# A state space stage reordered: ticks of small products and half a dense tile, with TensorE's order given by the source

## The chip, the cores and the metric

The kernel runs on one core of one Trainium2 chip. The metric is the device time of one execution in microseconds (us), as a median of several. Engines are named as the profile names them: PE (TensorE, the matrix unit), PEld (its weight loads), DVE (VectorE), ACT (ScalarE), POOL (GpSimd) and SP (the queue that issues nearly all DMA transfers). Differences under 0.2% can't be told from no change here.

## The reference

One layer of a decoder: a Mamba-2 state space branch and a sparse attention branch, joined by gates, then a squared-ReLU MLP, for a prompt of 16 + 512 tokens and for 8 decode sequences of 8 tokens each. The change concerns the state space branch and the projections that stand beside it:

```python
u = rmsnorm(h, norm1_w)
z, xbc, dt_raw, q, k, v, qi, ki, wi, g_ssm, g_attn = split_in(u @ w_in)
xbc, conv_state = causal_conv(xbc_raw, conv_prefix, conv_w, conv_b)   # width 4, then silu
...
def step(h, inp):                       # one chunk of 128 tokens, 4 groups of 8 heads
    xc, dc, bc, cc = inp
    acum = jnp.cumsum(dc * a_h, axis=1)
    decay = jnp.exp(jnp.where(causal, seg, -jnp.inf))
    cb = jnp.einsum('bign,bjgn->bijg', cc, bc)
    y = jnp.einsum('bijg,bijge,bjgep->bigep', cb, decay, xdt)
    y = y + jnp.einsum('bign,bgepn->bigep', cc, h) * jnp.exp(acum)[..., None]
    h = h * jnp.exp(last)[..., None, None] + jnp.einsum('bjge,bjgep,bjgn->bgepn', wj, xdt, bc)
...
y = (y + xs * d_skip) * jax.nn.silu(z)  # then a norm per group, times ssm_norm_w
merged = jax.nn.sigmoid(g_ssm) * (y_ssm @ w_ssm_proj) + jax.nn.sigmoid(g_attn) * (y_att @ w_attn_proj)
```

The decode sequences run the same recurrence from a given state (8 sequences, 32 heads, 64 x 128 each), which is read, used and written back updated.

## The kernel before

The 576 tokens and the 16 meta tokens lie in SBUF as normed activations split into a high and a low part (`uh`, `ul`, 8 x 128 rows of 592 columns). A dense tile is one block of 128 output columns of `w_in`: its weights come by DMA into `wr` (two buffers), ACT makes the high part `wh` (L128), POOL the low part `wl` by a subtraction (L129), and PE makes 2 halves of 24 products each (`mm3`, L151: 8 blocks of the contraction, three products high x high, low x high, high x low), one bank of PSUM (tag `w`, two banks) for each half of the columns.

Order: the order in which the source writes instructions gives priorities, and a scheduler of the framework then sets the order of every engine's instructions, and of SP's transfers, when the kernel is built. Each engine then runs its own list in order.

The stage in question makes, for each of four groups g of heads:

- six convolution tiles (`conv_tile`: B, C and four x tiles): the dense tile, copies by ACT into `rb` (L572 to L575), three multiply-adds by DVE (L588), tanh by ACT, two products by DVE (L593, L596), a scaled copy by ACT, transposes by PE (L608, L611), and stores to DRAM scratch (`d_bc`, `d_xd`, `d_x`, `d_b`);
- four `z` tiles (`z_tile`, silu by ACT and DVE L562, stored to `d_z`);
- `start(g)`: loads of that group's B, C and decode rows;
- four `states(g, i)`: a block `st` of decode states of 512 KB is loaded, transposed by PE (L682), multiplied by C (L690) and updated by POOL (L684), PE (L698) and DVE (L700);
- five `chunk(g, c)`, four of the prompt and one (c = 4) for decode and meta tokens: `bc` is loaded from `d_ac` by a broadcasting DMA and turned into the decay by ACT (L729, L731), PE makes the mask product (L734), DVE `cb` (L736) and eight products `bc` = decay x dt x cb (L741); PE makes the eight L743, the four L757 and the state update L768; then comes a chain DVE (L762, L763), POOL (L773), DVE (L774), ACT (L776), POOL (L777, L778), PE (L782), DVE and POOL (L160, L161, the root), DVE (L786), PE (L789), DVE (L791) and a store to `d_y`.

`Pipe` runs the units as generators: units of the next group's tiles are pushed beside the states and chunks of this group, first four states, then five chunks. `top_s()` (32 rounds of MAX8 and MATCH_REPLACE, L535 and L536, of a top-256) advances by two rounds beside each of these. `together` makes the first of a set of products wait for the operands of all of them. After the loop over groups, 16 gate tiles (`gate`, dense tiles with a tanh) follow, and then the next stage, attention on the decode sequences, with gathers of cached keys (`Kg`, L859) and the projection of `d_y` (`yw`, L1040).

## Time and profile before

| | us |
|---|---|
| median of 3 runs | 1550.33 |
| their range | 1547.67 to 1550.42 |
| the profiled execution | 1541.95 |
| its span, first to last instruction | 1540.2 |

| stage by its work | from to (us) | PE busy | DVE busy | POOL busy |
|---|---|---|---|---|
| up to the first convolution tiles | 0 to 165 | 143.6 | 135.9 | 54.4 |
| state space stage and gates | 165 to 745 | 522.5 | 405.8 | 329.0 |
| attention and merge | 745 to 1000 | 245.3 | 177.6 | 137.0 |
| output projection and MLP | 1000 to 1540 | 517.2 | 285.5 | 195.1 |

Busy time is the time in which the engine had an instruction in work. Matmuls overlap in the pipeline, so PE's busy time does not tell how far it is from its pace. A line such as `L151 PE MATMUL ... x915 | 282.1, 308 | 15.9 <-ACT rb L572` names line, engine, operation, count, busy time in us, mean ns of one, and the idle time ahead with what ended it. In the chain of waits each row has a start, a length and what took it.

### The profile page before, as it was taken

The numbers are of one execution on the slowest core, as the hardware profiler recorded it, in microseconds if no ns is written. First come the engines' busy times: TensorE is split into PE (matmuls) and PEld (weight loads), VectorE is DVE, ScalarE is ACT, GpSimd is POOL, SyncE is SP. The second block draws the span as 40 slices with busy tenths as digits, with TensorE's granted clock in tenths as the row PEclk, the third lists the DMA queues.
The fourth block names the chain that finished last, engine by engine and source line by source line (L and its number), as shares of the span: only waits on it lengthen the run. The fifth ranks groups of instructions, "written<-read, shape, count | busy, mean of one in ns | idle before, by whom it ended". The sixth has DMA issues, their size and how long they took to land.

```text
span 1540.2 us, 26573 instructions
## 1 busy us (share of the span) xinstructions
PE 1428.6 (93%) x9960; PEld 1290.4 (84%) x9960; DVE 1004.8 (65%) x1905; ACT 664.1 (43%) x1484; POOL 715.4 (46%) x644
## 2 busy tenths in 40 slices
PE   6899999888888898889899999989998999999998
PEld 6888989878878888779788887887897998899886
DVE  5799999878768676461444788864565644564444
ACT  4463445455555465443565565522342321232211
POOL 3422343647656566555445765244254533352322
PEclk9999999999999999999999999999999999999999
DMA  6424555786876877867984432035233312332212
GB/s 184 105 56 112 165 150 149 222 228 168 239 212 186 240 210 182 246 174 213 314 264 156 142 100 79 17 121 178 62 96 110 110 56 69 96 96 67 71 41 69
DMA packets 297609, 221.55 MB, mean 144 GB/s; under 512 B 43820, under 2 KB 267360, under 8 KB 297456
## 3 DMA queue, kind: packets, MB, share of 16 engines
q1 hardware_dynamic: 292232, 200.98, 46.1%
q0 software_dynamic: 5248, 18.88, 3.5%
q8 instruction: 78, 1.28, 0.3%
q14 instruction: 51, 0.42, 0.1%
HBM read 174.97 MB, written 44.07 MB: 142 GB/s over the span
## 4 chain that ended last, share of the span: by engine, by line
PE 51%; DVE 19%; DMA 13%; issue 6%; ACT 6%; POOL 4%; SPq 2%; POOLq 0%; DVEq 0%; ACTq 0%
PE s L1194 13%; PE w L151 12%; PE a L151 10%; PE w L1057 5%; DMA bc<-d_ac 3%; DVE ca L588 2%; DMA wr<-in_w_up_dram 2%; POOL wl L129 2%; DVE scs L536 2%; DVE m8s L535 2%; DVE bc L741 1%; DVE r L1218 1%; ACT wh L128 1%; DVE am L365 1%; DMA d_x<-tk 1%
## 5 line engine op out<-in xcount | busy, mean ns | idle before, releaser
L129 POOL TENSOR_TENSOR wl<-wr,wh 128x1024 fp32r<-128x1024 f32 x128 | 312.1, 2438 | 335.1 <-ACT wh L128 311.5
L151 PE MATMUL w<-uh,wh 128*128 128x288 f32 (+1 forms) x1168 | 360.6, 309 | 21.6 <-ACT rb L572 7.4
L151 PE MATMUL w<-ul,wh 128*128 128x288 f32 (+1 forms) x1168 | 355.7, 305 | 0.6 <-DVE ul L220 0.6
L151 PE MATMUL w<-uh,wl 128*128 128x288 f32 (+1 forms) x1168 | 355.0, 304 | 0.0
L151 PEld LDWEIGHTS w<-uh,wh 128*128 128x128 f32 x1168 | 224.8, 192 | 30.0 <-ACT rb L572 8.6
L151 PEld LDWEIGHTS w<-ul,wh 128*128 128x128 f32 x1168 | 224.9, 193 | 4.5 <-issue 2.9
L151 PEld LDWEIGHTS w<-uh,wl 128*128 128x128 f32 x1168 | 223.6, 191 | 2.1 <-issue 1.4
L128 ACT ACTIVATE wh<-wr 128x1024 fp32r<-128x1024 f32 x129 | 136.2, 1056 | 115.3 <-PE w L151 55.5
L129 POOL TENSOR_TENSOR dl<-wr,dh 128x1024 fp32r<-128x1024 f32 x40 | 99.0, 2477 | 158.1 <-ACT dh L128 157.9
L151 PE MATMUL a<-u2h,wh 128*128 128x288 f32 (+2 forms) x512 | 151.5, 296 | 1.0 <-ACT r L1217 1.0
L151 PE MATMUL a<-u2l,wh 128*128 128x288 f32 (+2 forms) x512 | 151.2, 296 | 0.0
L151 PE MATMUL a<-u2h,wl 128*128 128x288 f32 (+2 forms) x512 | 151.1, 295 | 0.0
L1196 DVE TENSOR_TENSOR h<-h,s 128x512 f32<-128x512 f32 (+1 forms) x101 | 67.3, 679 | 124.6 <-PE s L1194 124.2
L1194 PE MATMUL s<-dh,hh 128*128 128x512 f32 (+1 forms) x324 | 127.6, 395 | 6.3 <-DVE h L1196 6.3
L1194 PE MATMUL s<-dl,hh 128*128 128x512 f32 (+1 forms) x324 | 127.3, 394 | 0.0
L588 DVE SCALAR_TENSOR_TENSOR ca<-rb,cwT,ca 128x616 f32<-128x616 f32 x72 | 96.0, 1334 | 22.9 <-ACT ca L586 22.4
L1218 DVE TENSOR_TENSOR r<-r 128x288 f32<-128x288 f32 (+2 forms) x64 | 74.4, 1163 | 52.9 <-ACT r L1217 52.9
L128 ACT ACTIVATE dh<-wr 128x1024 fp32r<-128x1024 f32 x40 | 42.3, 1058 | 152.3 <-PE s L1194 131.3
L1194 PE MATMUL s<-dh,hl 128*128 128x512 f32 (+1 forms) x260 | 102.5, 394 | 0.0
L151 PEld LDWEIGHTS a<-u2h,wh 128*128 128x128 f32 x512 | 96.1, 188 | 2.1 <-ACT r L1217 1.5
L151 PEld LDWEIGHTS a<-u2l,wh 128*128 128x128 f32 x512 | 96.1, 188 | 0.7
L151 PEld LDWEIGHTS a<-u2h,wl 128*128 128x128 f32 x512 | 96.1, 188 | 0.0
(378 smaller groups left out, 3263.5 us busy)
## 6 DMA issues: line engine op xcount, KB each, us to landing
wr<-in_w_in_dram SPq DMA_DIRECT2D x64, 512.0 KB
wr<-in_w_up_dram SPq DMA_DIRECT2D x32, 512.0 KB
wr<-in_w_down_dram SPq DMA_DIRECT2D x32, 512.0 KB
st<-in_state_ssm_dram SPq DMA_DIRECT2D x16, 512.0 KB
bc<-d_ac SPq DMA_DIRECT2D x32, 256.0 KB
out_dram<-st SPq DMA_DIRECT2D x16, 512.0 KB
wr<-in_w_ssm_proj_dram SPq DMA_DIRECT2D x16, 512.0 KB
d_xd<-th SPq DMA_DIRECT2D x16, 296.0 KB
```

The costliest lines, as they stand in the source:

```text
L128: act.activation(hi, raw, AF.Copy)
L129: (lo_eng or pool).tensor_tensor(lo, raw, hi.bitcast(FT), op=OP.subtract)
L151: pe.matmul(ps[:, :c1 - c0], p[:, k, :], x[:, c0:c1], start=(k == 0 and i == 0), stop=(k == 7 and i == 2))
L365: dve.scalar_tensor_tensor(sc, r[:, :L], wis[:, t, h:h + 1], sc, op0=OP.mult, op1=OP.add)
L535: dve.max(m8, scs)
L536: dve.match_replace(scs, m8, scs, MARK)
L588: dve.scalar_tensor_tensor(ca[:, 0:616], rb[:, k:k + 616], cwT[:, 24 * k + ct:24 * k + ct + 1], ca[:, 0:616], op0=OP.mult, op1=OP.add)
L741: end = dve.scalar_tensor_tensor(mt, mt, dts[:n, c, 8 * g + hh:8 * g + hh + 1], cb[:n, :n], op0=OP.mult, op1=OP.mult)
L1057: pe.matmul(ps[:, :HQ], p[:, k, mc], x[k][:, c0:c1], start=(k == 0 and i == 0), stop=(k == 3 and i == 2))
L1194: pe.matmul(ps, x, w[:, cc], start=(k == 0 and i == 0), stop=(k == len(ws) - 1 and i == len(terms) - 1))
L1196: dve.tensor_tensor(h2[:, t, cc], h2[:, t, cc], ps, op=OP.add)
L1218: dve.tensor_tensor(r, r, r, op=OP.mult)
```

## The change

`inproj` of the tiles of this stage is cut in two by a new generator `dense`: weights are asked for (`w_load`), split two ticks later (`w_split`), and two ticks after that come the two halves, one in each tick, each evacuated by ACT right behind its 24 products. The loop counts ticks. In each tick first all running `states`, `chunk` and `start` units advance by a step, then the tiles whose step is not a half tile, then the one that has a half tile. A new tile starts every second tick, in the order conv and z of the four groups, then the 16 gates. The scan of group g begins at tick 33 + 20 g, with a new unit each second tick, in the order state, chunk, state, chunk, and so on, and `chunk(g, 3)` last. Inside the stage PE's instructions keep the order of the source (`manual_schedule` for PE alone); the other engines and SP's queue are still ordered by the scheduler. `together` is gone here. Loads are issued one to three ticks before their use, stores one or two ticks after their data. `top_s` yields after every round, two ticks in three up to tick 30 and one in four after. The meta tokens' state moves from `chunk(g, 4)` to `start(g)`, `cb` and `rd` share three buffers.

```diff
+    def dense(cols, n, evac):
+        raw = w_load(in_cols(cols))
+        yield from wait(2)
+        w = w_split(raw)
+        yield from wait(2)
+        for h in range(2):
+            ps = pst("w")
+            mm3(ps, w, uh, ul, h * n, h * n + n)
+            evac(h, ps)
+            yield
...
     with tc.tile_pool(name="p3", bufs=1, reuse_waits="tile") as p3, \
-            tc.tile_pool(name="p3s", bufs=1, reuse_waits="tile") as p3s:
+            tc.tile_pool(name="p3s", bufs=1, reuse_waits="tile") as p3s, \
+            tc.manual_schedule(engines={mybir.EngineType.PE}):
...
         def chunk(g, c):
...
-                sy.dma_start(bc[:n, :, :n], d_ac[None, h0:h0 + 4, 128 * c:128 * c + n].to_broadcast([n, 4, n]))
+                sy.dma_start(bc[:n, :, :n], d_ac[None, h0:h0 + 4, tok].to_broadcast([n, 4, n]))
+            yield from wait(2)
+            xd, EB = [p3.tile([128, 4, 128], FT, tag=x, name=x, bufs=2) for x in ("xd", "EB")]
...
+            for q, bc in enumerate(bcs):
                 for i in range(4):
                     act.activation(bc[:n, i, :n], bc[:n, i, :n], AF.Relu, scale=-1.0,
...
-            yield
-            py = pst("s")
             mts = [bcs[hh // 4][:n, hh % 4, :n] for hh in range(8)]
             for hh, mt in enumerate(mts):
-                end = dve.scalar_tensor_tensor(mt, mt, dts[:n, c, 8 * g + hh:8 * g + hh + 1], cb[:n, :n], op0=OP.mult, op1=OP.mult)
-            for hh, mt in enumerate(mts):
-                mm = pe.matmul(py[64 * (hh % 2):64 * (hh % 2) + 64, 128 * (hh // 2):128 * (hh // 2) + n],
-                               xt[:n, 64 * hh:64 * hh + 64], mt, start=True, stop=True)
-                if hh == 0:
-                    together(mm, [end])
+                dve.scalar_tensor_tensor(mt, mt, dts[:n, c, 8 * g + hh:8 * g + hh + 1], cb[:n, :n], op0=OP.mult, op1=OP.mult)
...
+            yield
...
+            py = pst("s")
+            for hh, mt in enumerate(mts):
+                pe.matmul(py[64 * (hh % 2):64 * (hh % 2) + 64, 128 * (hh // 2):128 * (hh // 2) + n],
+                          xt[:n, 64 * hh:64 * hh + 64], mt, start=True, stop=True)
...
+        line = []
+        for g in range(4):
             c = [conv_tile(ct) for ct in (16 + g, 20 + g, 4 * g, 4 * g + 1, 4 * g + 2, 4 * g + 3)]
             z = [z_tile(4 * g + j) for j in range(4)]
-            return [c[0], c[1], z[0], c[2], z[1], c[3], z[2], c[4], z[3], c[5]]
+            line += [c[0], c[1], c[2], z[0], c[3], z[1], c[4], z[2], c[5], z[3]]
+        line += [gate(gt, m) for gt in (0, 1) for m in range(8)]
+        scans = {}
+        for g in range(4):
+            base = 33 + 20 * g
+            scans.setdefault(base - 3, []).append(start(g))
+            for j, u in enumerate((states(g, 0), chunk(g, 0), states(g, 1), chunk(g, 1), states(g, 2), chunk(g, 2),
+                                   states(g, 3), chunk(g, 4), chunk(g, 3))):
+                scans.setdefault(base + 2 * j, []).append(u)
...
+        while line or scan or run or scans:
+            scan += scans.pop(tick, [])
+            scan = [u for u in scan if next(u, u) is not u]
+            if line and tick % 2 == 0:
+                run.append([-1, line.pop(0)])
+            for late in (False, True):
+                for x in run:
+                    if (x[0] + 1 in DENSE) == late and x[1] is not None:
+                        if next(x[1], x) is x:
+                            x[1] = None
+            run = [[x[0] + 1, x[1]] for x in run if x[1] is not None]
+            if tick % 3 < 2 if tick < 30 else tick % 4 == 0:
                 next(tops, None)
+            tick += 1
```

The count of matmuls on PE is the same in both programs. Line numbers after the change are larger: L626 stands for L588, L639 for L593, L811 and L814 for L736 and L741, L830 for L743, L851 for L782, L858 for L789, L865 for L798, L935 for L859, L1133 for L1057, L157 and L134 for L151 and L136.

What DVE has in its list around the end of the top-k, before (L535 and L536 are its rounds, L541 and L545 what follows the last one, L700 the update of a state, L736 the first chunk):

```order
L535 MAX m8s<-scs 128x8
L593 SCALAR_TENSOR_TENSOR rb<-th,ca 128x528
L596 SCALAR_TENSOR_TENSOR rb<-th,ca 128x64
L588 SCALAR_TENSOR_TENSOR ca<-rb,cwT,ca 128x616
L536 MATCH_REPLACE scs<-m8s,scs 128x1032
L588 SCALAR_TENSOR_TENSOR ca<-rb,cwT,ca 128x616
L541 TENSOR_SCALAR nm<-scs 128x8
L545 TENSOR_SCALAR scs<-scs 128x1024
L562 SCALAR_TENSOR_TENSOR zt<-zt,zl 128x576
```

And after, at the same place (L541 and L542 are the rounds now, L546 and L550 what follows them):

```order
L639 SCALAR_TENSOR_TENSOR rb<-th,ca 128x528
L642 SCALAR_TENSOR_TENSOR rb<-th,ca 128x64
L542 MATCH_REPLACE scs<-m8s,scs 128x1032
L541 MAX m8s<-scs 128x8
L542 MATCH_REPLACE scs<-m8s,scs 128x1032
L546 TENSOR_SCALAR nm<-scs 128x8
L550 TENSOR_SCALAR scs<-scs 128x1024
L547 TENSOR_TENSOR nm_6543<-nm,cst 128x64
```

All 32 rounds stand ahead of the first chunk in both lists, with 6 tiles through L593 (L639) by the last round in both; between there and the first `cb` stand 3 more before and 4 more after.

DVE at a chunk in the middle of the stage, before: after the eight products (L741) come convolution steps of the next group, one after the other, with the chain of two chunks between them.

```order
L736 TENSOR_TENSOR cb<-a,cst 128x128
L741 SCALAR_TENSOR_TENSOR bc<-bc,dts,cb 128x128 x8
L786 TENSOR_SCALAR rd<-cst,ss 128x128
L791 SCALAR_TENSOR_TENSOR y_3741<-y_3741,nwT,a 128x128 x4
L160 TENSOR_SCALAR ss<-a 128x1
L588 SCALAR_TENSOR_TENSOR ca<-rb,cwT,ca 128x616
L762 TENSOR_TENSOR y_4068<-s,EB 128x512
L588 SCALAR_TENSOR_TENSOR ca<-rb,cwT,ca 128x616
L786 TENSOR_SCALAR rd<-cst,ss 128x128
L763 TENSOR_TENSOR y_4068<-y_4068,s 128x512
L771 TENSOR_TENSOR hn<-hn,s 128x512
```

After, the same engine and place; L763 is the update of a state (L700 before):

```order
L763 TENSOR_TENSOR st<-st,s 128x512 x2
L844 TENSOR_TENSOR y_3950<-y_3950,sz 128x512
L626 SCALAR_TENSOR_TENSOR ca<-rb,cwT,ca 128x616
L166 TENSOR_SCALAR ss<-a 128x1
L626 SCALAR_TENSOR_TENSOR ca<-rb,cwT,ca 128x616
L855 TENSOR_SCALAR rd<-cst,ss 128x128
L626 SCALAR_TENSOR_TENSOR ca<-rb,cwT,ca 128x616
L811 TENSOR_TENSOR cb<-a,cst 128x128
L814 SCALAR_TENSOR_TENSOR bc<-bc,dts,cb 128x128 x8
L639 SCALAR_TENSOR_TENSOR rb<-th,ca 128x528
```

A state's update and the steps of one convolution tile now stand between any two chunks; before, all four states of a group stood ahead of its chunks.

PE at the end of the stage, before: the last products of the scan (L789, L798) stand among gate tiles; behind these rows come 188 more dense products with six L873 between them, and then the next stage's transposes of `Kg` (L873).

```order
L151 MATMUL w<-uh,wh 128x288
L789 MATMUL a<-rd,cst 128x128
L798 MATMUL a<-cst,hn 128x128 x4
L151 MATMUL w<-ul,wh 128x288
L151 MATMUL w<-uh,wl 128x288
```

After, the same place, from the last dense product of the stage on (`ysh` and `ysl` are the halves of `yw`; L949 are the transposes of `Kg`):

```order
L157 MATMUL w<-uh,wl 128x288
L858 MATMUL a<-rd,cst 128x64
L851 MATMUL a<-cst,xd 128x1
L858 MATMUL a<-rd,cst 128x128
L865 MATMUL a<-cst,hn 128x128 x4
L1133 MATMUL w<-ysh,wh 128x288 x2
L949 MATMUL s<-cst,Kg 128x128 x8
L1133 MATMUL w<-ysl,wh 128x288
```

No dense product is left behind the scan's last ones; the products of the next stage follow them at once.

More of the change, by code (lines that the diff above doesn't have):

```diff
@@ new lines, in conv_tile @@
+        ps = pst("a")
+        pv = ps.rearrange("p (k n) -> p k n", k=4)
+        for c in range(4):
+            pe.transpose(pv[:, c, :], dst[:, 80 + 128 * c:208 + 128 * c], idf)
+        act.copy(tk[:, 0:4, :], pv)
+        ps = pst("a")
+        pe.transpose(ps[:80, 0:128], dst[:, 0:80], idf)
+        act.copy(tk[:80, 4, :], ps[:80, 0:128])
+        yield from wait(2)
+        dd = d_x[:, 128 * ct:128 * ct + 128] if ct < 16 else d_b[:, 128 * (ct - 16):128 * (ct - 15)]
+        sy.dma_start(dd[0:512].rearrange("(t p) c -> p t c", p=128), tk[:, 0:4, :])
@@ L825, in body @@
-        scan.run()
-    for gt in (0, 1):
-        for m in range(8):
-            gate(gt, m)
+            line += [c[0], c[1], c[2], z[0], c[3], z[1], c[4], z[2], c[5], z[3]]
[7 more added lines that the diff above has]
+                scans.setdefault(base + 2 * j, []).append(u)
```

271 lines of the change are left out of this document (146 added, 125 removed).

## The prediction

> **What bounds the kernel now.** I read the page first, then busy time by stage, the chain of waits through the stage that is rewritten, and the single lines of DVE and POOL in it.
>
> ```profile
> PE 1428.6 (93%) x9960; PEld 1290.4 (84%) x9960; DVE 1004.8 (65%) x1905; ACT 664.1 (43%) x1484; POOL 715.4 (46%) x644
> ```
>
> PE looks full over the whole span. Matmuls overlap in the records, though, so a busy PE is not a PE at its pace. The pace is read from runs on the chain (start, us, what):
>
> ```profile
> 149.81 20.51 PE w L151 x153
> ...
> 692.68 1.09 PE s L743 x16
> 693.77 1.09 PE s L757 x8
> 694.86 0.86 PE s L768 x2
> ```
>
> A dense product takes 20.51 / 153 = 0.134 us. Small ones take between 0.068 us (L743 alone) and 0.117 us (the three rows, 26 products in 3.04 us). The stage runs from the first convolution tiles (172.5) to the last dense product (743), and I cut it at the first L736, the start of the first chunk. Of each stretch: all work, then L151 alone.
>
> ```profile
> 172.50:316.00 143.50, 132.29 (x995) 127.39 (x994) 126.59 (x149) 70.86 (x167) 68.47 (x70) 0.98 0.62 179
> 316.00:743.00 427.00, 380.66 (x2963) 348.17 (x2963) 271.01 (x492) 216.90 (x525) 256.12 (x242) 0.98 0.75 211
> 172.50:316.00 143.50, 122.00 (x844) 117.05 (x842) 0.98 0.62 179
> 316.00:743.00 427.00, 289.32 (x1900) 265.39 (x1898) 0.98 0.75 211
> ```
>
> Columns after the length are busy PE, PEld, DVE, ACT, POOL (the lower two rows have PE and PEld only), then clock, DMA share and GB/s. In the first stretch DVE is the bound: 126.6 of 143.5 us. At 0.134 us a dense and 0.082 us a small product (my choice between 0.068 and 0.117, nearer the low end because the many narrow products are the cheap kind), PE's own pace is 844 x 0.134 + 151 x 0.082 = 125 us there, and 1900 x 0.134 + 1063 x 0.082 = 342 us in the second stretch, which lasted 427. So 18 + 85 us are the most a better order of PE can bring, out of 570.5. What uses up the 85 us is spread thin:
>
> ```profile
> PE a L682 <- DMA st<-in_state_ssm_dram: 8.1, 5, 3.5
> PE w L151 <- ACT rb L572: 7.4, 5, 4.2
> ...
> PE s L743 <- DVE bc L741: 4.1, 5, 1.6
> ...
> L729 ACT ACTIVATE bc<-bc,acum 128x128 f32<-128x128 f32 (+1 forms) x160 | 48.6, 379 | 59.2 <-DMA bc<-d_ac 59.0
> ```
>
> No wait of PE is large, each follows another engine. ACT stood 59 us at the transfers that fill bc, and the evacuations that PE waits for (L572) stand behind that in ACT's queue.
>
> The rows that matter most are these, of DVE and POOL (least, median and largest duration in ns; rows with bars have the total, the mean and the idle time ahead):
>
> ```profile
> L588 DVE SCALAR_TENSOR_TENSOR ca<-rb,cwT,ca x72: 834/860/3894, 191.7 to 596.5; 128x616 f32<-128x616 f32 x72
> L535 DVE MAX8 m8s<-scs x32: 1210/1226/1237, 150.6 to 278.0; 128x8 f32<-128x1032 f32 x32
> L741 DVE SCALAR_TENSOR_TENSOR bc<-bc,dts,cb x160: 268/341/3123, 316.1 to 692.2; 128x128 f32<-128x128 f32 x128, 64x64 f32<-64x64 f32 x32
> L741 DVE SCALAR_TENSOR_TENSOR bc<-bc,dts,cb 128x128 f32<-128x128 f32 (+1 forms) x160 | 66.1, 477 | 0.7
> L736 DVE TENSOR_TENSOR cb<-a,cst x20: 209/276/292, 315.8 to 686.9; 128x128 f32<-128x128 f32 x16, 64x64 f32<-64x64 f32 x4
> L593 DVE SCALAR_TENSOR_TENSOR rb<-th,ca x24: 684/704/3743, 199.6 to 598.2; 128x528 f32<-128x528 f32 x24
> L562 DVE SCALAR_TENSOR_TENSOR zt<-zt,zl x16: 734/1020/2959, 209.2 to 583.7; 128x576 f32<-128x576 f32 x16
> L774 DVE TENSOR_TENSOR y<-y,sz x20: 409/684/1517, 326.2 to 697.9; 128x512 f32<-128x512 f32 x16, 128x256 f32<-128x256 f32 x4
> L129 POOL TENSOR_TENSOR wl<-wr,wh x128: 2352/2394/3343, 20.2 to 1463.5; 128x1024 fp32r<-128x1024 f32 x128
> L129 POOL TENSOR_TENSOR wl<-wr,wh 128x1024 fp32r<-128x1024 f32 x59 | 144.8, 2454 | 105.8 <-ACT wh L128 98.8 <-DMA wr<-in_w_in_dram 4.0 <-PE a L682 2.9
> ```
>
> The same L588 takes 0.83 us or up to 3.9. Where it is long, POOL is in a subtraction (DVE's row first, then POOL's, twice):
>
> ```profile
> 248.12 2.25 DVE L588 SCALAR_TENSOR_TENSOR ca<-rb,cwT,ca 128x616 f32<-128x616 f32 x1
> 247.32 2.40 POOL L129 TENSOR_TENSOR wl<-wr,wh 128x1024 fp32r<-128x1024 f32 x1 [1.87 <-ACT wh L128]
> 218.76 3.85 DVE L588 SCALAR_TENSOR_TENSOR ca<-rb,cwT,ca 128x616 f32<-128x616 f32 x1
> 219.56 2.39 POOL L129 TENSOR_TENSOR wl<-wr,wh 128x1024 fp32r<-128x1024 f32 x1
> ```
>
> Both times L588 ends 0.65 us after POOL's 249.72 and 221.95, about its own undisturbed length: it waited POOL out. I therefore treat POOL's work and DVE's operations with two operands in SBUF as one resource, used by turns. MAX8, which reads one tile, never stretches (1210 to 1237).
>
> The Trainium skill, page "SBUF — State Buffer", section "Who interferes with whom", says the same as a rule: a VectorE instruction with two SBUF inputs and a GpSimd instruction that reads SBUF exclude each other for a whole instruction, whichever came first. The trace agrees (3.85 against 0.83 us). By that rule the saving comes out at 18 us, as in the sum below; were the two free of each other, at 54 us, as in the rival "PE's pace".
>
> **The change part by part.** No product, copy or DMA is added or removed; all is order, plus two small changes of buffers.
>
> 1. *First stretch, up to the first chunk.* The rounds of the top-k (L535 with its match) were to be spread out, but in DVE's row order all 32 still stand ahead of the first chunk. Ten convolution tiles come before that chunk instead of nine. DVE's 126.6 of 143.5 us leave at most 17 us to win, at least 0; I take 6, since DVE must also do one more tile. PE stands at 77 remaining half tiles then (1900 / 24 = 79 before): even.
>
> 2. *Middle and end, 77 ticks of one half tile each* (ticks 39 to 115; a group's scan begins every 20 ticks). Per 20 ticks PE needs 20 x 24 x 0.134 + (1214 / 4) x 0.082 = 89 us. The shared resource needs: on DVE 18 x 0.860 + 6 x 0.704 + 4 x 0.734 + 40 x 0.341 + 5 x 0.684 = 39.6 us; on POOL 10 x 2.394 = 23.9, and the rest of a group, (68.5 + 256.1 - 144.8 - 8 for the gathers) / 4 = 43, some of it waiting. Together 106; I take 104. While convolution tiles and scans run together (to tick 85) that is the bound, 46 x 5.2 = 239 us; then gates and the last scan at PE's pace, 31 x (3.22 + 1.25) = 139 us. Sum 378. To this comes what an in-order PE loses beside a full neighbour: between 0 and 13% (the 12% by which DVE missed filling the first stretch, its own bound); I take half, 6%, or 23 us. 401 against 427: 26 us saved, ends 49 and 0. What this removes is the alternation in the old order between four states (little for DVE) and five chunks (much). The bc transfers issued two ticks ahead of their use, the evacuation after each half and the waits on sets of eight (`together`) are inside these 26 us. So is SP's queue: bc, xd and the weights stand there behind stores (d_y, st, d_xd) that hold the queue until their data are done; the new source issues each store one or two ticks after its data, so these should hold it less, and I count nothing for it because ACT, who waits for bc, is not the bound. If that cover goes, ACT's 59 us come back as late evacuations, of which PE felt 7.4 before. DMA goes from 0.75 to 0.75 x 427 / 401 = 0.80 busy.
>
> 3. *The tail.* PE's row order ends with a half tile, then four groups of small products, then the next stage. Before, the last chunk's chain ran under dense work:
>
> ```profile
> 696.61 8.67 PE w L151 x65
> 705.28 0.11 PE a L782 x2
> 705.39 5.20 PE w L151 x38
> ...
> 713.02 3.18 DMA d_y<-y
> ...
> 717.01 12.04 DMA Kg<-in_cache_k_dram,idx
> ...
> 753.71 5.61 DMA yw<-d_y
> ```
>
> ```profile
> 705.43 0.16 DVE L160 TENSOR_SCALAR ss<-a 128x1 f32<-128x1 f32 x1 [6.88 <-PE a L782]
> 708.05 0.29 DVE L786 TENSOR_SCALAR rd<-cst,ss 128x128 f32<-128x128 f32 x1 [2.46 <-POOL ss L161]
> 711.57 1.12 DVE L791 SCALAR_TENSOR_TENSOR y<-y,nwT,a 128x128 f32<-128x128 f32 x4 [3.24 <-PE a L789]
> 705.12 2.38 POOL L129 TENSOR_TENSOR wl<-wr,wh 128x1024 fp32r<-128x1024 f32 x1 [2.79 <-ACT wh L128]
> 707.46 0.55 POOL L161 TENSOR_TENSOR ss<-ss,cst 128x1 f32<-128x1 f32 x1
> ```
>
> From the product at 705.28 to the landed Kg at 729.04 it is 23.8 us, all covered by gate tiles. These gate tiles now stand inside the scan, so the cover is gone. Left of the 23.8: about 5 us from the sum of squares to d_y (0.16 + 2.38 + 0.55 + 0.29 + 0.2 for L789 + 1.12 = 4.7, POOL's subtraction still standing between), then yw is loaded in 5.6 us without waiting for Kg, and split. The first product of the next stage starts some 13 us after PE's last half tile and is followed at once by one that needs Kg. I take 14 us lost, between 8 and 24.
>
> A gap has one more price. In a stretch with long stalls the granted clock (the third number from the right) is below 1:
>
> ```profile
> 520.00:560.00 40.00, 35.48 (x291) 31.93 (x290) 26.96 (x46) 20.05 (x52) 19.42 (x17) 0.91 0.78 228
> ```
>
> The Trainium skill, page "TensorE: Matmul & The Clock Gate", section "What's actually happening", says that PE falls to half its clock after an idle window of some 3.4 us and needs about as long under load to come back. By that rule the tail's gap costs an estimated 3.4 / 2 = 1.7 us more and the saving is 16 us; the sum does without it.
>
> Sum: -6 - 26 + 14 = -18. The profiled execution took 1541.95 us (its span 1540.2), 8.4 below the median 1550.33 of the runs; 1542 - 18 = 1524, which on the median is 1532.
>
> **The rivals.** *PE's pace* (faster still): DVE and POOL do not exclude each other enough to matter, and the middle runs at 77 x 4.47 = 344 us plus 6%, 365, saving 62. With the same 6 and 14 the sum is -54, 1496. For it: DVE and POOL each had idle time in the second stretch (271 and 256 of 427). Against: the stretched L588.
>
> *PE waits for its eight* (slower): between the product L734 that starts a chunk's mask and the products L743, PE now has one half tile, the rank-one product and the four of L757 to do, 3.22 + 0.2 + 1.09 = 4.5 us, in fixed order. DVE needs 0.28 + 8 x 0.341 = 3.0 when free, 0.28 + 66.1 / 20 = 3.6 at the mean that the trace has, 4.5 with a convolution step of 0.86 beside them, as its new row order has it, and 6.9 if that meets one whole subtraction of POOL (2.39). Before, PE filled such waits with any dense product that was ready. At 6.9 the wait is 2.4 us, and what DVE is behind from earlier ticks comes on top; at 4 us for each of the 16 full chunks it is 64 us instead of the 23 that I allow: +41 - 18 = +23, 1573. It decides from (23 + 18) / 16 = 2.6 us a chunk on. For it: DVE and POOL are the fuller pair in this stretch. Against: the trace of before has only 4.1 us of PE waiting for bc.
>
> *No effect*: the alternation smooths little, and PE loses 11% beside the full pair, 378 x 1.11 = 419; the middle then saves 8, the first stretch 6, and the tail takes the 14 back: 1550, give or take 3.
>
> **How the numbers follow.** Forecast (1515 to 1545) 0.50, PE's pace 0.15, waits for its eight 0.25, no effect 0.10. Faster by over 0.2% (3 us, about what this measurement can tell): 0.50 + 0.15 = 0.65; the same 0.10; slower 0.25. The likeliest time is 1532. The range reaches down to the faster rival, 1495, and up into the slower one, 1570; half of that rival and a little below 1495 are left out.
>
> **What would show it.** Right: L736's first start between 300 and 316; the stretch from there to the last L151 near 400 us, with POOL's and DVE's waits about as long in sum but evenly spread; a gap on PE of 10 us or more right before the next stage, with Kg or yw as the releaser. Wrong: many waits of PE at the chunk's products on DVE's bc, each over 3 us (then the slower rival); DVE idle by a third in the middle while PE has no waits (then PE's pace); the first chunk after 325 us, or a tail without a gap (then the terms 6 and 14 are off).

## The result: 1.2% slower, and the profile after

The changed kernel took 1567.7 us (median of 4 runs, 1561.2 to 1569.8) against 1549.0 us (1545.4 to 1550.4) of the kernel before: a ratio of 1.0117 with a 95% interval of 1.0082 to 1.0153. The forecast was 1532 us, a gain of 18; the time lies near the upper end of the stated range, 1495 to 1570 us. All ratios below are to runs of the kernel before on the same chip as the run they belong to; traces are of one execution each, and a median can lie up to 9 us from its trace. The profiled execution of the changed kernel has a span of 1568.0 us against 1540.2. These 27.8 us are 9 more than the medians differ by (18.7): the profiled execution before, 1541.95 us, lies 7 us under its median. So a few us between two single traces, in the tables below too, are not yet a result.

Busy time by stage after, in the prediction's columns, cut at the first chunk's `cb` and at the last dense product of the stage:

```profile
172.50:337.00 164.50, 139.29 (x997) 134.49 (x996) 131.16 (x153) 77.86 (x174) 71.17 (x76) 0.97 0.56 157
337.00:738.00 401.00, 374.32 (x2949) 344.01 (x2947) 239.14 (x478) 209.15 (x505) 253.06 (x224) 0.96 0.76 211
738.00:800.00 62.00, 44.14 (x312) 34.71 (x313) 23.04 (x58) 28.23 (x61) 26.80 (x26) 0.78 0.88 280
```

| piece | before | after | difference | forecast |
|---|---|---|---|---|
| 172.5 to the first `cb` | 143.5 | 164.5 | +21 | -6 |
| to the last dense product (before: to 743, the prediction's cut) | 427 | 401 | -26 | -26 |
| to the next stage's first scores (L881, now L957) | 0 | 27 | +27 | +14 |
| to the end | 797.2 | 803.0 | +6 | 0 |

By the prediction's cuts the middle gained what was forecast, and the gain reappeared as loss ahead of it and behind it. In the trace of before, though, the last dense product ends at 739.6 us; 743, where the prediction has it, is the start of the next stage's first scores. Cut at the same event on both sides, the middle went from 424 to 401 us (-23) and the tail from 3 to 27 (+24). What PE waited for after the change, from 172 to 765 us (line, what it waited for: total us, times, longest):

```profile
PE s L635 <- POOL r L631: 20.6, 14, 6.7
PE a L851 <- POOL xd L848: 12.0, 2, 6.0
PE a L858 <- DVE rd L855: 9.6, 3, 5.8
PE a L661 <- DVE rb L639: 7.8, 5, 2.5
PE w L1133 <- ACT ysh L128: 7.3, 1, 7.3
PE a L755 <- ACT sT L749: 4.6, 6, 2.1
PE w L1133 <- POOL ysl L129: 4.2, 1, 4.2
```

L635 is the transpose of 27 rows of a convolution tile (L580 before). In the fixed order it stands right ahead of a dense half, and its input is copied by POOL (L631, L632) behind the 2.4-us subtraction of weights:

```profile
189.67 2.38 POOL L129 TENSOR_TENSOR wl<-wr,wh 128x1024 fp32r<-128x1024 f32 x1
191.99 0.76 POOL L632 COPY r<-rb 128x3 f32<-128x3 f32 x1
192.69 0.20 POOL L631 COPY r<-rb 128x24 f32<-128x24 f32 x1
```

The waits of PE in the first stretch after (172 to 337 us), and the same transpose in the whole stage before:

```profile
PE s L635 <- POOL r L631: 17.2, 9, 6.7
PE a L661 <- DVE rb L639: 7.8, 5, 2.5
```

```profile
PE s L580 <- DVE y L762: 0.7, 1, 0.7
PE s L580 <- POOL r L577: 0.7, 1, 0.7
```

The tail, from the chain of waits (start, us, what):

```profile
734.46 3.28 PE w L157 x23
...
744.85 4.63 DMA d_y<-y
750.37 11.46 DMA Kg<-in_cache_k_dram,idx
761.88 1.98 PE s L949 x8
...
765.01 3.71 PE s L957 x8
```

The last dense product ends at 738; the last chunk's store, the gather behind it and eight transposes follow one by one with PE nearly idle. The granted clock, in 40 slices of 39 us, shows it as the one 6:

```profile
PEclk9999999999999999999699999999999999999999
```

**Where the time sits, by PE alone.** From 172 us to the first scores, overlapping records counted once, I split the trace into time with no product running (idle), half of the product time that ran while half the clock was granted (its cost), and the rest, the products at full clock:

| 172 us to the first scores | length | idle | cost of half clock | products |
|---|---|---|---|---|
| before | 570.9 | 57.5 | 10.4 | 503.0 |
| after | 593.0 | 69.5 | 20.7 | 502.8 |
| difference | +22.1 | +12.0 | +10.3 | -0.2 |

The products cost the same in sum. By the windows of busy PE, idle time went from 11 to 25 us in the first stretch, from 46 to 27 in the middle, and from nothing to 18 in the tail. Products moved as well: the first stretch has 5.7 us more of them (914 dense ones, before 844), the middle 11.0 less and the tail 5.0 more, so 11 of the middle's 26 us are work that is done elsewhere. And idle time got lumpier: before, PE's longest gap in the stage was 4.2 us; after, there are gaps of 6.7, 6.0, 6.0 and 5.8 us, inside each of which 6.8 to 10.2 us at half clock begin, and one of 7.3 us within a stretch of 27.3 us at half that had begun behind a gap of 3.6. In all 23.9 us of the stage before were at half clock, and 63.7 after.

### The profile page after: what moved, and what is told of

It is laid out like the page before. It is cut to its first block, busy times and chain, and to the rows that moved or that the text cites. A ratio compares the mean times of both kernels' runs of the same rounds, so it can differ in the third digit from the quotient of the medians.

```text
span 1568.0 us, 26635 instructions
## 1 busy us (share of the span) xinstructions
PE 1440.5 (92%) x9960; PEld 1302.5 (83%) x9960; DVE 982.2 (63%) x1905; ACT 670.1 (43%) x1484; POOL 719.6 (46%) x644
## 4 chain that ended last, share of the span: by engine, by line
PE 53%; DMA 8%; DVE 7%; POOL 4%; ACT 4%; issue 2%; SPq 0%; POOLq 0%; DVEq 0%; ACTq 0%
PE w L157 13%; PE s L1270 13%; PE a L157 10%; PE w L1133 5%; POOL wl L129 2%; DMA wr<-in_w_up_dram 2%; DMA bc<-d_ac 2%; ACT wh L128 1%; DVE r L1294 1%; PE s L957 1%; PE s L830 1%; PE a L983 1%; PE s L949 1%; DVE P L1081 1%; DMA tgs<-d_g 1%
## 5 line engine op out<-in xcount | busy, mean ns | idle before, releaser
L157 PE MATMUL w<-uh,wh 128*128 128x288 f32 (+1 forms) x1168 | 364.2, 312 | 6.2 <-ACT qis L336 4.1
L157 PE MATMUL w<-ul,wh 128*128 128x288 f32 (+1 forms) x1168 | 353.9, 303 | 0.6 <-DVE ul L226 0.6
L157 PE MATMUL w<-uh,wl 128*128 128x288 f32 (+1 forms) x1168 | 354.2, 303 | 0.0
L157 PEld LDWEIGHTS w<-uh,wh 128*128 128x128 f32 x1168 | 227.6, 195 | 10.7 <-ACT qis L336 4.5
L157 PEld LDWEIGHTS w<-ul,wh 128*128 128x128 f32 x1168 | 227.4, 195 | 2.4 <-issue 1.2
L157 PEld LDWEIGHTS w<-uh,wl 128*128 128x128 f32 x1168 | 225.8, 193 | 0.1
L157 PE MATMUL a<-u2h,wh 128*128 128x288 f32 (+2 forms) x512 | 151.5, 296 | 0.6 <-ACT r L1293 0.6
L157 PE MATMUL a<-u2l,wh 128*128 128x288 f32 (+2 forms) x512 | 151.2, 296 | 0.0
L157 PE MATMUL a<-u2h,wl 128*128 128x288 f32 (+2 forms) x512 | 151.1, 295 | 0.0
L626 DVE SCALAR_TENSOR_TENSOR ca<-rb,cwT,ca 128x616 f32<-128x616 f32 x72 | 90.4, 1255 | 51.8 <-ACT ca L624 51.1
L157 PEld LDWEIGHTS a<-u2h,wh 128*128 128x128 f32 x512 | 96.1, 188 | 1.5 <-ACT r L1293 0.8
L157 PEld LDWEIGHTS a<-u2l,wh 128*128 128x128 f32 x512 | 96.1, 188 | 0.7
L157 PEld LDWEIGHTS a<-u2h,wl 128*128 128x128 f32 x512 | 96.1, 188 | 0.0
```

What stands on the lines that cost most here:

```text
L157: pe.matmul(ps[:, :c1 - c0], p[:, k, :], x[:, c0:c1], start=(k == 0 and i == 0), stop=(k == 7 and i == 2))
L626: dve.scalar_tensor_tensor(ca[:, 0:616], rb[:, k:k + 616], cwT[:, 24 * k + ct:24 * k + ct + 1], ca[:, 0:616], op0=OP.mult, op1=OP.add)
```

## The experiments

Theories are named by letter as they came up. The table has the ratio and, from the trace and in us, the stage by PE's time as above, the tail (start of the last dense product to the first scores) and the start of the last chunk's mask product.

| kernel | ratio (95%) | 172 to scores | idle | half clock | products | tail | last mask |
|---|---|---|---|---|---|---|---|
| before | 1 | 570.9 | 57.5 | 10.4 | 503.0 | 3.6 | 685 |
| after | 1.0117 (1.0082 to 1.0153) | 593.0 | 69.5 | 20.7 | 502.8 | 27.4 | 725 |
| e1 free order | 1.0141 (1.0107 to 1.0176) | 587.2 | 47.0 | 16.8 | 523.4 | 26.7 | 720 |
| e2 transpose later | 1.0132 (1.0098 to 1.0167) | 595.8 | 62.7 | 31.4 | 501.7 | 27.3 | 728 |
| e3 two tiles held | 1.0149 (1.0113 to 1.0185) | 584.1 | 63.9 | 17.1 | 503.1 | 14.8 | 714 |
| e5 no alternation | 1.0277 (1.0244 to 1.0310) | 599.9 | 74.9 | 15.1 | 509.9 | 27.4 | 729 |
| e7 five held | 1.0099 (1.0067 to 1.0131) | 588.1 | 67.0 | 15.7 | 505.5 | 3.6 | 705 |
| e9 five last | 1.0196 (1.0148 to 1.0244) | 591.3 | 64.9 | 23.8 | 502.6 | 2.6 | 714 |
| e8 gates behind, free | 1.0105 (1.0056 to 1.0153) | 579.9 | 41.7 | 10.8 | 527.4 | 16.3 | 710 |
| e4 added products | 1.0143 (1.0095 to 1.0191) | 588.5 | 59.6 | 13.8 | 515.1 | 15.8 | 717 |
| e10 free, pairs together | 1.0052 (1.0028 to 1.0075) | 577.6 | 58.0 | 14.3 | 505.3 | 38.4 | 712 |
| e13 and gates paced | 1.0092 (1.0059 to 1.0125) | 575.7 | 56.1 | 18.6 | 501.0 | 2.7 | 695 |
| e18 three paced, Bz on ACT | 1.0085 (1.0050 to 1.0120) | 575.3 | 56.4 | 14.9 | 504.0 | 14.0 | 700 |
| e6 Bz on ACT | 1.0096 (1.0062 to 1.0130) | 587.1 | 66.3 | 19.0 | 501.7 | 27.5 | 719 |
| e14 e10, keys first | 1.0089 (1.0047 to 1.0130) | 571.7 | 53.5 | 17.6 | 500.6 | 39.9 | 704 |
| e15 e14, Bz on ACT | 1.0075 (1.0047 to 1.0102) | 576.0 | 54.9 | 19.2 | 501.9 | 28.9 | 709 |
| e16 after, keys first | 1.0136 (1.0105 to 1.0167) | 588.9 | 70.7 | 15.0 | 503.2 | 26.9 | 721 |
| e17 before, keys first | 1.0051 (1.0028 to 1.0074) | 574.4 | 57.5 | 13.6 | 503.4 | 3.6 | 688 |
| e12 before, alternating | 1.0251 (1.0197 to 1.0305) | 604.4 | 81.5 | 19.7 | 503.1 | 29.4 | 729 |
| e19 the same, state by group | 1.0176 (1.0131 to 1.0220) | 590.8 | 68.7 | 20.9 | 501.2 | 27.4 | 711 |

### The fixed order undone, and what went with it

```diff
-            tc.tile_pool(name="p3s", ...) as p3s, \
-            tc.manual_schedule(engines={mybir.EngineType.PE}):
+            tc.tile_pool(name="p3s", ...) as p3s:
```

> The changed kernel with one thing undone: TensorE's order in the stage is left to the scheduler again; ticks, early loads and the alternation stay. Theory A (the fixed order carries the loss, the loads and the alternation carry the gain): the waits of the 27-row transpose L635 for POOL's r (20.6 us) go, the first masked product of the stage comes back from 337 to about 316 us, the tail between the last dense product and the first scores shrinks from 27 to under 10 us, and the middle keeps its 401 us: 1567.7 - 21 - 20 = about 1527 us. Theory B (the fixed order itself made the middle's gain of 26 us): first stretch and tail recover and the middle goes back to 427: about 1550 us. Above 1568 would mean that the order is not what lost.

No theory held. The first stretch did come back (first mask at 312 us) and idle time fell by 22 us, but products cost 20 us more and the total stayed. The rows of the eight products of a chunk (busy us, mean ns; the changed kernel, then this run):

```profile
L830 PE MATMUL s<-bc,xt 128*64 128x128 f32 (+1 forms) x320 | 21.1, 274 | 0.0
```

```profile
L829 PE MATMUL s<-bc,xt 128*64 128x128 f32 (+1 forms) x320 | 36.8, 285 | 5.4 <-DVE bc L813 5.3
```

The mean hardly differs, the busy time by 15.7 us. Neighbours of these narrow products go to different halves of the output rows and start some 7 ns apart, side by side. In the changed kernel the sixteen records of a chunk (two for each product) stand in one piece; in the free order the scheduler had set other products between them (start, us, what; the chain of the changed kernel, then the timeline of this run):

```profile
728.98 1.02 PE s L830 x16
```

```profile
337.76 0.44 PE L829 MATMUL s<-bc,xt 128*64 128x128 f32 x4
338.13 0.44 PE L747 MATMUL a<-cst,st 128*128 128x128 f32 x2
338.50 0.44 PE L829 MATMUL s<-bc,xt 128*64 128x128 f32 x4
338.87 1.12 PE L839 MATMUL s<-xw,Bt 128*128 128x512 f32 x2
```

That small products on different column groups run at once is what the Trainium skill, page "TensorE: Matmul & The Clock Gate", section "Part 3: Packing small matmuls — row/col tiling", says; the 7 ns agree. But pairs that were parted are the smaller part of the loss: in this run 111 of 160 pairs still start within 12 ns of each other, in the changed kernel 154. The larger part goes with the changes between narrow and full-width products. From the start of the last narrow product to the next, a full-width one, it is 0.20 us, and from a full-width one to the first narrow one 0.28, against 0.11 between two full-width products of 128 columns; this run has 63 pieces of L829 and so 63 changes each way, the changed kernel 20. By these numbers an estimate of the loss is 43 x 0.3 = 13 us for the changes and 43 x 0.1 = 4 for the pairs. The change had removed, with the scheduler's order, the two dependencies (`together`) that kept each eight in one piece, so this run was no clean undoing. With them put back:

```diff
-                pe.matmul(py[64 * (hh % 2):...], xt[...], mt, start=True, stop=True)
+                mm = pe.matmul(py[64 * (hh % 2):...], xt[...], mt, start=True, stop=True)
+                if hh == 0:
+                    together(mm, [end])      # end: the last of the eight on DVE; likewise in states()
```

> The run with the free order once more, with the two dependencies put back that hold the eight masked products, and the eight products with the transposed states, in one piece (the change had taken them out with the scheduler's order). Theory D (the free order alone gained 18 us of waits in the first stretch and lost 16 us because the eight products, two of which run side by side when they are neighbours, were pulled apart: 36.8 us for 320 products instead of 21.1): they take 21 to 23 us again, and the stage falls by about 14 us: profile about 1546 us, ratio to the kernel before 1.001 to 1.006, the tail of 26 us still there. Rival (the products' own time was hidden): as with the free order alone, ratio 1.012 to 1.016.

```profile
L831 PE MATMUL s<-bc,xt 128*64 128x128 f32 (+1 forms) x320 | 21.3, 277 | 15.4 <-DVE bc L815 15.4
```

Theory D held in its main terms: 21.3 us, products back at 505, the ratio 1.0052 with an interval below that of the changed kernel. (The stage fell by 9.6 us, not by 14, and the tail is 38 us, not 26.) So the fixed order costs about 0.65% (by the two intervals 0.2 to 1.1%), 10 us, some half of the loss. Its one benefit, the eights in one piece, the kernel before had as well, by `together`. What is left of the loss has no shown cause; by the traces it is 6.7 us in the stage and 5.5 behind it, sizes in which single traces differ. Idle time in the stage is that of before (58.0 and 57.5), but in another shape: the dense products end at 711 us, the tail is 38 us, and the clock is at half for 30.7 us in one piece. The 6.7 us are 3.9 of half clock, 2.3 of products and 0.5 of idle time.

### One wait taken away in the fixed order

```diff
+        yield
         po = pst("s")
         pe.transpose(po[:27, 0:128], r27, idf)
...
         act.copy(ro, po[:27, 0:128])
-        ...
-        yield
```

> The changed kernel with the 27-row transpose L635, its eviction and its transfers one tick later, nothing else. Theory A (PE stands behind POOL's queue at that transpose, some 1.5 us a tile): the waits for r (20.6 us from 160 to 790 us, 17.2 of them before the first masked product) go, and the first stretch falls from 164.5 to about 148 us: 1548 to 1554 us. Rival (the first stretch is bound by what VectorE and POOL do there, the transpose only shows it): the wait passes to the next instruction in the fixed order, L661 behind VectorE's conv steps, and the total moves by less than 5 us: 1563 to 1568 us.

The rival held. L635's waits are gone, and the next product in the fixed order waits twice as long as before for DVE (7.8 us in the changed kernel):

```profile
PE a L661 <- DVE rb L635: 16.6, 6, 4.8
```

(L635 is here a line of the convolution's end.) In this trace the first chunk did come 7 us earlier and idle time fell to 62.7 us, but half clock rose to 31.4. The ratio did not move beyond its interval. Taking POOL's burst at the group starts away:

```diff
-                pool.tensor_tensor(G.Bz[:, q], Bs[...].to_broadcast(...), K("in32")[...].to_broadcast(...), op=OP.mult)
+                for k in range(4):
+                    act.activation(G.Bz[:, q, k], Bs[:, q].bitcast(FT), AF.Copy, scale=K("in32")[:96, k:k + 1])
```

> The changed kernel with one edit: each group's Bz (two POOL products of 1.3 us at the group's start) is made by eight small ScalarE copies with a scale. Theory (the three stalls of about 6.3 us at the group starts, and the half clock behind each, come from POOL's queue, in which Bz and the weighted rows stand ahead of the chunk's sums L847 and L848): each stall shrinks by the 2.6 us, and where it falls under about 4 us the clock stays up: 8 to 18 us less in the middle, ratio to the kernel before 1.000 to 1.007. Rival (the stall is the other POOL work and VectorE's share of it, or it passes to L858 and L755): within 3 us of the changed kernel, ratio 1.010 to 1.014.

Two of the three stalls shrank from 6.0 to 2.7 us and half clock behind them from 6.8 to 3.4, so the place is right; the middle was 6 us shorter. The clock did not stay up, as expected under 4 us, and the ratio's interval overlaps the changed kernel's. Inconclusive in size.

### Dense work moved behind the scan

```diff
-            if line and tick % 2 == 0:
+            if line and tick % 2 == 0 and tick not in (98, 106):
```

> The changed kernel with no dense tile started in ticks 98 and 106, so that the last two gate tiles run four ticks later, beside the end of the last chunk. Theory A (the tail of 27 us is short of dense work, and runs at half clock for that): the four half tiles (about 3 us each at full clock) cover the last chunk's chain, the clock stays up, and the tail falls from 27 to about 12 us while the middle ends at the same time: 1550 to 1556 us. Rival (in the last group too the stage is held by VectorE and POOL, or the ticks without a dense half stop on waits that it hid): the dense products end some 12 us later with the same tail behind them: 1564 to 1572 us.

The same with ticks (84, 90, 96, 102, 108):

> The changed kernel with no dense tile started in ticks 84, 90, 96, 102 and 108: five gate tiles run later, five of their ten halves behind the last product of the scan. Theory B, formed after the first four runs (from 172 us to the last dense product every kernel so far took 561 to 573 us, however PE's order was set; what the change lost is the tail, because the gates that used to lie behind the scan now run out before it): the dense part stays at 565 to 570 us, the tail from the last dense product to the first scores falls from 27 to about 5 us, the rest is 800 us: about 1545 us, a ratio to the kernel before of 0.998 to 1.004. Rival (the ticks without a dense half stand on VectorE and POOL, so the dense part grows by what the tail loses): 1562 to 1570 us, ratio 1.010 to 1.016.

The same five tiles in one piece behind the last tick:

> The same five gate tiles, all put behind the last product of the scan (240 dense products in a row), so that the last ten ticks of the scan have no dense half. Theory B: what those ticks lose to waits is bounded by the chunk's own chain; if PE was the bound there they shrink from 5.4 to about 2.5 us each and nothing is lost: dense part 566 to 572, tail about 3 us, total 1541 to 1548 us. Rival (a tick without dense work lasts as long as with it, because each product waits for VectorE or POOL): the dense part grows by about 25 us and the total is 1565 to 1572 us.

The tail did what theories A and B said, 27 to 15, 4 and 3 us; the time did not follow. Idle time fell only from 69.5 to 64 to 67. With five tiles spread, PE stands in the ticks without a dense half at a wait that the changed kernel has 12.0 us of:

```profile
PE a L851 <- POOL xd L848: 21.0, 4, 6.8
PE s L635 <- POOL r L631: 20.5, 14, 6.2
```

So the rivals are nearer: e3 is inside its rival's range, e7 (1558 us) between its two, and e9 (1575 us) even above its rival's. That fits a chunk's own chain through DVE and POOL that shows wherever no dense work lies over it. The two dependencies of e10 kept, with the same five tiles held and each gate's first product tied to the mask of one chunk earlier:

```diff
+            if paced and h == 0:
+                together(mm, ready[-2:-1])     # ready: the evictions of the mask products so far
```

> The run before this one, and the gates held back: no dense tile starts in ticks 84, 90, 96, 102, 108, and each gate's first product depends on the masked product's eviction one chunk earlier, so that the scheduler can't draw the gates ahead. Theory D: on top of the 14 us of the pairs the tail's 20 us go, since dense products stand behind the scan's end, with the waits that a free order avoids: 172 us to the first scores about 560 us, total 1525 to 1533 us, ratio 0.988 to 0.994, a version that beats both. Rival (what the tail loses the dense part gains, as with five tiles held in the fixed order): 1540 to 1548 us, ratio 0.997 to 1.004.

> The free order with the pairs together, Bz on ScalarE, and three gate tiles held back (ticks 90, 98, 106; each gate's first product depends on the masked product's eviction one chunk earlier). Theory F (idle time of TensorE is set by the scan's chain through VectorE and POOL, 53 to 58 us of it in every order with the pairs together; moving gates only moves it): 172 us to the first scores 570 to 576 us, total 1548 to 1556 us, ratio 1.001 to 1.008. Rival (with three tiles and the burst gone both the tail and the waits shrink): first scores at 735 to 740 us, total 1535 to 1542 us, ratio 0.992 to 0.998.

Neither gained: idle 56.1 and 56.4 us, the stage 575.7 and 575.3, as theory F said of the second. Both totals, 1559.6 and 1559.7 us, lie above every range given; by the traces the part behind the stage took 810 us in both, 13 more than before. All sixteen gates written behind the stage, order free but without the pairs:

> The changed kernel with TensorE's order left to the scheduler and all sixteen gate tiles written behind the stage, as in the kernel before; ticks, early loads and alternation stay. In the resulting order the scheduler still draws the gates into the last two groups as filler, and only 36 dense products stand behind the last product of the scan. Theory B: dense part about 561 us as in the run with the free order, tail 27 less 5 us, rest 800: about 1555 us, ratio 1.006 to 1.010. Rival (gates behind the stage are enough, since the scan ends earlier when its products go first): tail under 6 us, 1535 to 1540 us, ratio 0.992 to 0.997.

Idle time was the least of all (41.7), products the dearest (527.4), as in e1. The ratio, 1.0105, is just above theory B's range, the total, 1561.9 us, 7 above its value. And work added, 24 dense products of 288 columns in each of the four last ticks, unused:

```diff
+            if not line and not any(x[0] <= 5 for x in run) and tick >= 114:
+                mm3(pst("w"), last_w[0], uh, ul, 0, HQ)
```

> The changed kernel with 24 more dense products (288 columns, result unused) in each of the four ticks of the scan that have no dense half at its end: work added, none taken away. Theory C (a good part of the tail's price is TensorE's clock, 27 us at half): the clock stays at 1.0 until about 755 us, the eight products L949 x8 and L957 x8 take 0.9 and 2.0 us instead of 2.0 and 3.7, and the total falls by 4 to 7 us: 1560 to 1563 us, ratio 1.006 to 1.009. Theory B (the tail is the chain last chunk, d_y, gather of Kg, scores; the clock is a small part of it): within 3 us of the changed kernel: 1565 to 1570 us.

Half clock began at 751 us instead of 742 and lasted 13.7 us instead of 27.3, and the first scores came 4.5 us earlier. But this trace was ahead before the first added product, by 6 us at the 2500th dense product from 172 us on (686.6 against 692.6), by 7 at the last mask; from the kernel's own last dense product to the scores it has some 29 us, as against 27. The eight L957 (L961 here) took 3.7 us as before, where theory C had 2.0. The timed runs agree with theory B: 1565.7 us is in its range, and the ratio's interval lies above theory C's 1.006 to 1.009. So these products gained nothing. What the clock alone costs in the tail stays open, since it was at half again when the scores came.

### The chain behind the last chunk

```diff
-    with tc.tile_pool(name="p2s", ...) as p2, tc.tile_pool(name="p2k", ...) as p2k:
+    with tc.tile_pool(name="p2k", ...) as p2k, tc.tile_pool(name="p2s", ...) as p2:
```

Kg then lies over other tiles than the one that the last store reads; no product moves.

> The run with the free order and the pairs together, and one edit behind the stage: the pool of the gathered keys and values is opened ahead of the samples' other pool, so that Kg lies over tiles that are done with the last chunk's products, not over the tile that the last transfer reads. Theory E (what is left of the loss is the chain last chunk, transfer out of y1's tile, gather of Kg, scores): the gathers go at about 721 us instead of 734, the first scores start at 736 to 739 instead of 750, total 1539 to 1544 us, ratio 0.993 to 0.999. Rival (the gather stands behind the chunk's own POOL work, or KcT and P now wait for the same transfer): the first scores at 747 to 751, ratio 1.003 to 1.008.

> The changed kernel with the same one edit (the pool of the gathered keys and values opened first), order fixed as it is. Theory E: the gathers leave before the last transfers, the tail falls from 27 to 14 to 18 us: 1553 to 1558 us, ratio 1.003 to 1.007. Rival: the tail stays at 25 us or more, ratio 1.010 to 1.014.

> The kernel before with the same one edit. Theory E: there dense products run until 3.6 us before the first scores, so the chain is covered and nothing is won: within 0.3% of the kernel before. Rival (the gather's late start costs the kernel before as well): 5 us or more faster, ratio under 0.997.

> The free order with the pairs together, the gathered keys' pool first, and Bz made on ScalarE instead of POOL. Theory (POOL's burst at the group starts holds up the chunk in flight, whatever the order): 3 to 8 us less than without it, 1533 to 1540 us, ratio 0.990 to 0.995. Rival (a free order has dense products to issue there, so nothing is won): as the run without it.

Theory E fell. The gathers left early, and the loads of `yw`, which had taken 5.6 us in the kernel before, took their place on the chain (e14; `L1136` is the projection, L952 the transposes of `Kg`):

```profile
722.89 12.15 DMA yw<-d_y
...
736.85 11.98 DMA yw<-d_y
...
751.08 1.33 PE w L1136 x4
752.41 1.71 PE s L952 x8
```

The first scores came 4 to 6 us earlier and nothing was left of it in the ratio; the kernel before got 0.5% slower. Bz on ScalarE made no difference that can be told (1.0075 and 1.0089).

### Alternation by itself

```diff
-            for j, u in enumerate((states(g, 0), chunk(g, 0), states(g, 1), ..., chunk(g, 4), chunk(g, 3))):
+            for j, u in enumerate((states(g, 0), ..., states(g, 3), chunk(g, 4), chunk(g, 0), ..., chunk(g, 3))):
```

> The changed kernel with one thing undone: in each group the four state units come first, then chunk 4 and chunks 0 to 3, as in the kernel before; the fixed order and the early loads stay. Theory A (the middle's gain of 26 us comes from alternating states and chunks, which evens out what VectorE and POOL have to do): the stretch from the first masked product to the last dense one goes from 401 to 420 to 427 us, the total to about 1588 us. Rival (the gain comes from the fixed order with a dense half behind each wait, and from loads that are issued early): 401 us stay, 1565 to 1571 us.

1.6% slower than the changed kernel, as theory A's total, but not at theory A's place: the first mask came at 362 us, since four state units go first, and the stretch behind it was 383 us. The trace shows 12 of the 25 us. In the kernel before, alone:

```diff
-                scan.push(states(g, j) if j < 4 else chunk(g, (4, 0, 1, 2, 3)[j - 4]))
+                scan.push((states(g, j // 2) if j % 2 == 0 else chunk(g, j // 2)) if j < 7 else chunk(g, (4, 3)[j - 7]))
```

> The kernel before with one part of the change alone: in each group the units alternate (states 0, chunk 0, states 1, ... chunk 4, chunk 3), with the carried state's first product moved into the group's start; order left to the scheduler, no ticks. Theory D (alternation is the change's one gain: undoing it cost 18 to 24 us): 1520 to 1530 us, ratio 0.984 to 0.992. Rival (the alternation only matters in a fixed order, where a run of chunks has nothing else to issue; a scheduler that draws dense products into the gaps has evened it out already): 1540 to 1548 us, ratio 0.997 to 1.003.

That kernel let a group's last chunk use the next group's carried state. With the state kept by group:

> The kernel before with the units of each group alternating, the carried state kept by group (the earlier run of this edit let a group's last chunk carry the next group's state). Theory (alternation needs loads that are issued ticks ahead, which the kernel before does not have; the wrong state at the seam cost little): 1575 to 1590 us, ratio 1.018 to 1.028. Rival (the seam made that run slow; alternation gives what undoing it cost in the changed kernel): 1520 to 1530 us, ratio 0.984 to 0.992.

Alternation, with the two small parts of the change that came with it here (the meta tokens' product at the group's start, three buffers shared by `cb` and `rd`), makes the kernel before slower, 1.0176. By the trace its dense products end 4 us earlier (735 against 739), but the last group's five masks, at 644, 647, 660, 671 and 685 us before, now start at 644, 663, 686, 707 and 711, and the tail is 27.4 us as in the changed kernel. So the uncovered tail comes with the spreading of the chunks, not only with the gates' place. That early loads are what makes alternation pay, as expected there, is not shown: ACT waited 59.0 us for bc before and 58.3 after. No run has the ticks and early loads in a free order without alternation, so how much of the 0.52% that e10 still loses is the alternation's stays open.

## Why the prediction was wrong, point by point

- *What bounds it.* "18 + 85 us are the most a better order of PE can bring" put down to order all that its pace left over. Of these 103 us only 57.5 were idle and 10.4 the cost of half clock; the products at full clock took 503 us in either order, where 0.134 and 0.082 us give 467. With 0.134 for a dense product a small one took 0.11, near the upper end of the 0.068 to 0.117 that the prediction chose from. And the idle time was not all order: in the free orders made from the changed kernel with the eights together 53 to 58 us stayed idle. There, moving dense work moved the idle time and did not lessen it; that the scan's chain through DVE and POOL sets the amount is not shown, since no run made that chain shorter, and with 68.7 us in e19, also a free order with the eights together, the order of the units counts too.
- *First stretch, -6: this term failed, +21.* It asked what DVE would have left, and put PE's rank in order at nothing. DVE did not fill the stretch (131 of 164.5 us); PE stood 25 us in it at two transposes behind POOL and DVE. Of the 21 us, 14.0 are idle time, 1.3 half clock and 5.7 products, among them 70 more dense ones, which the prediction saw as 77 remaining half tiles for 79 and called even. The forecast's own test, the first `cb` after 325 us, shows that the term failed. e1 and e10 bring the first mask back to 312, so the fixed order is the cause; the one transpose that e2 moved accounts for 7 us of it in that trace and for nothing in the time.
- *Middle, -26: as forecast by its own cut* (-23 by the same event), 401 us, but partly by luck. The 23 us allowed for an in-order PE came to 26.7 us idle and 12.3 of half clock. What was to set the pace was DVE and POOL by turns, 104 us for each 20 ticks, with PE at 89. The trace has steps of 108 us from group to group, and PE's products alone, at full clock, fill 96, 97 and 92 of the three. The third step is as long as the second although convolution ends at 582 us and DVE has a third less to do:

```profile
445.00:553.00 108.00, 99.48 (x785) 91.19 (x785) 76.58 (x141) 64.22 (x159) 72.75 (x69) 0.97 0.80 222
553.00:661.00 108.00, 99.18 (x756) 91.15 (x755) 51.84 (x112) 50.27 (x119) 63.14 (x49) 0.92 0.77 210
```

  So PE was nearer its own bound than the forecast had it, and the sum came out right although a small product was priced too low. What the forecast missed besides is that this gain is not independent of the other terms: idle time left the middle by 19.6 us and came back by 31.6 outside it.
- *Tail, +14: mis-sized, 27.* The chain was named rightly, but yw was taken to fill PE early. In the order, Kg's transposes and the products of yw stand among each other, and both were late (11.5 us for the gather, 7.3 and 4.2 us of waits for yw's split). The clock's price was 6.7 us, 4.4 of it ahead of the scores: 27.3 us at half, in which PE had products only now and then (it was busy for 9.4 of the tail's 27 us). That this sparseness kept the clock down is not tested. From the window of some 3.4 us in the Trainium skill, page "TensorE: Matmul & The Clock Gate", section "What's actually happening", the prediction had an estimate of 1.7 us. The trace agrees with the 3.4 us (every stretch at half is a multiple of it), but gaps of 2.1 and 2.5 us were followed by half clock too.
- *The rest, 0: +5.8*, by PE's time 3.0 idle and 5.4 half clock less 2.6 of products. The runs don't settle it; it was 795 to 814 us across the kernels, and 810 in e17, whose source differs from the kernel before only in the order of two pools.
- *The rivals.* "PE waits for its eight" has the sign and nearly the time (1573), but not the mechanism: L830 does not appear among PE's waits after. PE's waits were in the places that the fixed order puts ahead of the dense halves, the tiles' transposes, the sums of squares (L851, L858). That is what the rival should have been: any small product with a queue behind it, not the one that waited most before. "PE's pace" had nothing for it.

## What to carry to other kernels

Split the time of the bound engine into idle, half clock and work, over the whole stage to the next stage's first instruction, before adding up gains by stretch: a gain in one stretch that leaves idle time unchanged in sum is a move, not a gain. In a fixed order, look at what each small product waits for on the other engine's queue, not at what it waited for when a scheduler could fill the gap. Few long waits can cost more than the same idle time in many short ones: in the stage before and after, each gap over 3 us brought a stretch of half clock or stood in one; of those between 1.5 and 2.6 us 5 of 15 did.

## What the runs showed of the hardware

Two things were not expected. Narrow products that go to different halves of the output rows are dear when full-width products stand between them: 320 records took 21.1 to 21.3 us of busy time in pieces of sixteen and 36.8 in 63 pieces, and at each change between the two kinds 0.2 to 0.3 us passed between the starts. And the load of yw, 5.6 us in the kernel before, took 12.2 and 12.0 us when it was issued right behind the gathers (e14; 10.2 and 11.6 in e16), so that their earlier start was paid by the loads.
